# Second projections of a hybrid decoder trunk: all sums and low parts on VectorE, four of seven products' residuals on ScalarE and accumulating DMAs

## The chip, the core and the metric

The kernel runs on one core of one Trainium2 chip. The core has five engines that run their own instruction streams in order: TensorE (PE, with its weight loads shown apart as PEld), VectorE (DVE), ScalarE (ACT), GpSimd (POOL) and SyncE (SP, which here only issues DMAs). The metric is the device time of one execution in microseconds (us); lower is better. A profile is one execution of its own, with a span and times of single instructions.

## The reference

One sequence of 1024 tokens with 1024 features goes through two layers in float32. Each layer is a token mixer and a SwiGLU feed-forward network (FFN), each with an RMSNorm and a shift, scale and gate from the conditioning vector. The first mixer is a sparse attention with top-k keys, the second a gMLP.

```
for layer in range(2):
    h = modulate(rmsnorm(x, norm_mix_g[layer]), sh1, sc1)
    y = dsa_mixer(h, ...) if layer == 0 else gmlp_mixer(h, ...)      # both end in  "... @ w_o" / "y @ w_out"
    x = x + g1[:, None, :] * y
    h = modulate(rmsnorm(x, norm_ffn_g[layer]), sh2, sc2)
    x = x + g2[:, None, :] * ((silu(h @ w_gate) * (h @ w_up)) @ w_down)
return rmsnorm(x, final_g)
```

The change concerns the four *second projections* and the residual that follows each: `@ w_o` (1024 to 1024) of the attention, `@ w_down` (2816 to 1024) of the two FFNs, and `@ w_out` (2048 to 1024) of the gMLP, each with `x + gate * (...)`.

## The kernel before, in words

Activations are kept transposed: features on the 128 partitions, tokens along the row, in two chunks of 512 tokens. `x1` is eight tiles of 128x1024, one for each 128 output features.

**The second projections** all run through `out_win` (L1009). It computes a matrix product by Strassen's method in Winograd's form: the inner dimension, the output features and the tokens are each halved, and seven products take the place of eight. The inner dimension is cut into pieces: one piece of 4 for the attention (`[4]`), `[4, 4, 3]` for each FFN and `[4, 4]` for the gMLP; a piece of n covers 2n blocks of 128 inner features. For each piece, the seven products run in the order 1, 2, 6, 7, 4, 5, 3 (`ORD`, L1129). Each product has four output tiles (m = 0 to 3) of 128x512.

Precision is kept by splitting each operand in a high and a low part (`split`, L1056): ScalarE rounds to the high part, another engine subtracts it from the source to get the low part, and each block is three matmuls (`mm3`, L176: high by high, high by low, low by high). Product 2 of the first piece is an exception in the FFNs and the gMLP (`RAW_F`, L1106): it takes unsplit float32 operands. So a product of a piece of 4 is 4 x 4 x 3 = 48 matmuls of 128x512, and one of a piece of 3 is 36.

Ahead of the matmuls of a product come `mv_prep` (L1076, the moving side, from `graw` tiles) and `w_prep` (L1102, the weights, from `wraw` tiles). Between them they make, in a piece of 4: 28 low parts for the moving side and 28 for the weights (4 for each product), 16 sums for the moving side and 16 for the weights (all for products 6 and 7 and what follows from them). That is 88 subtractions or additions of 128x512 with both sources in SBUF, L1058 being all the low parts and L1084 to L1126 the sums. The tables at L88 to L91 say which of them go to GpSimd: `GS_P` and `WS_P` (indices whose sums do, moving side and weights), `GL_P` and `WL_P` (indices whose low parts do). With the values before, GpSimd takes 33 of the 88 and VectorE 55.

After the four output tiles of a product, the residual is added (`residual`, L950): VectorE reads the PSUM tile, multiplies by the gate and adds to the right eighth of `x1`. A product has four of these, a piece 28. Which part of `x1` a product goes to is told by `DST` (L1130): products 1 and 2 to features 0 to 511 of the first token chunk, 6 and 3 to the same features of the second chunk, 7 and 5 to features 512 to 1023 of the second chunk, 4 to those of the first. Products 1, 6, 7 and 4 share one group of four PSUM tiles (`X`), which goes on accumulating: TensorE may not write product 6 into a tile before the residual of product 1 has read it. Products 2 and 5, 3 use another group (`Z`).

Work is put on the engines in the order of the program text, rearranged by the framework's scheduler. Loads go on SP's DMA queue: the next piece's raw tiles are issued at products 4, 5 and 3 (`AHEAD`, L87). The weights' split tiles (`wst`) have eight buffers, so two products' worth: ScalarE can round the weights of a product only as TensorE ends the one two before. The pool `tmp` holds the short-lived 128x512 tiles named by `t2` (L132), four buffers.

The next stage's statistics and norm are interleaved with the last piece (L1170, L1334 and the like), and the first products of the next FFN or gMLP with that.

Of the kernel before, what the change touches and what calls it, by code (L numbers as in the profile page):

```python
# [14 lines left out]
AF = mybir.ActivationFunctionType  # L15
ALU = mybir.AluOpType
# [68 lines left out]
FIRST = ['13', '12', '11', '10', 'A0', 'A2', 'A3', 'A1', 'x0', 'x2', 'x3', 'x1', '21', '20', '23', 'p1', '22', 'B1', 'B0', 'B2', 'B3', 'x4', 'x6', 'x5', 'x7']  # L85
FIRST_O = ['13', '10', '11', 'A2', 'A3', 'x0', 'x3', 'A1', '12', 'x2', 'A0', 'x1', 'p1', '20', '23', 'B3', '21', 'B1', '22', 'B2', 'B0', 'x5', 'x4', 'x7', 'x6']
AHEAD = {4: [("A", i) for i in range(4)], 5: [("1", i) for i in range(4)], 3: [(w, i) for w in "2B" for i in range(4)]}  # L87
GS_P = (1,)  # L88
GL_P = (0, 2)
WS_P = (0, 2)  # L90
WL_P = (1,)  # L91
FM2 = (3,)
FORD = (6, 1, 7)
DGW = 1
# [19 lines left out]
def trunk(ctx, tc, xT, c, modT, vec, kgb, w_idx, w_q, w_a, wuk, wuv, wo, wg, wu, wd,  # L114
          bwu, bwv, bwo, bws, bbs, outT):
    nc = tc.nc
    PE, DVE, ACT, POOL, SP = nc.tensor, nc.vector, nc.scalar, nc.gpsimd, nc.sync
# [2 lines left out]
    pg = ctx.enter_context(tc.tile_pool(name="pg", bufs=37))  # L120
    wrp = ctx.enter_context(tc.tile_pool(name="wrp", bufs=2))
    wsp = ctx.enter_context(tc.tile_pool(name="wsp", bufs=8))
    tmp = ctx.enter_context(tc.tile_pool(name="tmp", bufs=4))
    sm = ctx.enter_context(tc.tile_pool(name="sm", bufs=4))
    psa = ctx.enter_context(tc.tile_pool(name="psa", bufs=4, space=PSUM))
    psb = ctx.enter_context(tc.tile_pool(name="psb", bufs=4, space=PSUM))
# [5 lines left out]
    def t2(name, dt=F32):  # L132
        return tmp.tile([P, CW], dt, name=name, tag="t2")
# [239 lines left out]
    for t in BEG:  # L373
# [8 lines left out]
        elif t[0] in "ab":  # L382
            k, ch = int(t[1]), int(t[0] == "b")
            cs = slice(ch * CW, ch * CW + CW)
# [77 lines left out]
    gate = [None]  # L462
# [90 lines left out]
    for ch in range(2):  # L553
        p = pa("kn_ps")
# [27 lines left out]
    for ch in range(2):  # L582
        p = pa("kT_ps")
# [363 lines left out]

    x1 = [None] * KT

    def residual(ps, xk, ch, gate, src=None):  # L950
        cs = slice(ch * CW, ch * CW + CW)
        DVE.scalar_tensor_tensor(xk[:, cs], ps, gate, (xk[:, cs] if src is None else src), op0=ALU.mult, op1=ALU.add)  # L952

    g_d = drm.tile([FT, P, T], F32, name="g_d")
# [54 lines left out]
    def out_win(src, wsrc, gate, x, pieces, xsrc=None, first=None, hook=None):  # L1009
# [66 lines left out]
        def mv_prep(pi, j):  # L1076
# [3 lines left out]
            for i in range(n):  # L1080
                (b11, b12), (b21, b22) = halves(pi, "1", i), halves(pi, "2", i)
                s = {1: b11, 2: b21, 7: b12, 4: b21, 5: b11, 3: b22}.get(j)
                if j == 6:
                    eng(GS_P, i).tensor_sub(b11, b12, b11)  # L1084
                    s = hold(("g", i)) if late else t2("gs")
                    eng(GS_P, i).tensor_sub(s, b22, b11)  # L1086
                if j == 7:
                    eng(GS_P, i).tensor_sub(b12, b22, b12)  # L1088
                if late and j == 4:
                    eng(GS_P, i).tensor_sub(b21, b21, keep.pop(("g", i)))  # L1090
                if j in whole(pi):
                    r.append(s)
                else:
                    t = pg.tile([P, 2, CW], F32R, name="gm", tag="pg")
                    r.append(split(t, s, CW, eng(GL_P, i)))
                if j == 6 and late:
                    keep["g", i] = s
                elif j == 6:
                    eng(GS_P, i).tensor_sub(b21, b21, s)
            return r  # L1100

        def w_prep(pi, j):  # L1102
# [3 lines left out]
            for m in range(4):  # L1106
                (a11, a22), (a12, a21) = halves(pi, "A", m, n), halves(pi, "B", m, n)
                s = {1: a11, 2: a12, 7: a11, 4: a22, 5: a21, 3: a12}.get(j)
                if j == 6:
                    eng(WS_P, m).tensor_sub(a11, a11, a21)  # L1110
                    s = (hold(("w", m)) if late else tmp.tile([P, CW], F32, name="wsum", tag="wt", bufs=2))[:, :n]
# [20 lines left out]
        def run():  # L1132
            fetch(len(todo))
            for pi, n in enumerate(pieces):
                last = pi == len(pieces) - 1
                if last:
                    for q in SQP:
                        sqpg[q] = page("sqp")
                        POOL.memset(sqpg[q][:, 0:1], 0.0)
                X = [pa("d_ps") for _ in range(4)]  # L1140
                Z = None
                for o, j in enumerate(ORD):
                    prep(pi, j)
                    if o < 6:
                        prep(pi, ORD[o + 1])
                    if last and o == 4:
                        prep(pi, 3)
                    if not last:
                        for what, i in AHEAD.get(j, ()):
                            if what in "AB" or i < pieces[pi + 1]:  # L1150
                                load(pi + 1, what, i)
                        if j == 3:
                            prep(pi + 1, 1)
                    if j in (2, 5):
                        Z = [pb("d_ps") for _ in range(4)]
                    mv, w = pre[pi, j]
                    mo, ch = DST[j]
                    for m in range(4):
                        p = (X if j in (1, 6, 7, 4) else Z)[m]
                        with (tc.issue_after(pe_chain[LOCK[n][j, m]].ins) if last and (j, m) in LOCK[n] else ExitStack()):  # L1160
                            for k in range(n):
                                first, end = k == 0 and j in (1, 2, 5), k == n - 1 and j in (2, 3, 4)
                                if j in whole(pi):
                                    PE.matmul(p, w[m][k], mv[k], start=first, stop=end, skip_group_check=j != 2)
                                else:
                                    mm3(p, w[m][k], mv[k], first, end, j != 2)
                        residual(p, x[m + mo], ch, gate[:, m + mo:m + mo + 1])
                    if hook is not None:
                        hook()
                    if last and j == 4:  # L1170
                        yield 0
            yield 1
# [428 lines left out]
    for ch in F1:  # L1601
        if ch is None:
            continue
        cs = slice(ch * CW, ch * CW + CW)
# [5 lines left out]
        for k in range(KT):  # L1610
            o = page("o")[:, :CW]
            x, fg = x1[k][:, cs], V[:, V_FIN + k:V_FIN + k + 1]
# [69 lines left out]
```

## Time and profile before

| | us |
|---|---|
| median of 3 runs (2596.45 to 2601.98) | 2601.79 |
| the profiled execution's own time | 2602.36 |
| its span | 2600.7 |

| second projection | stretch of the span, us | pieces |
|---|---|---|
| attention output | 525 to 645 | [4] |
| first FFN, down | 1084 to 1290 (its edges run from 1074 to 1317) | [4, 4, 3] |
| gMLP output | 1733 to 1890 (from 1721 to 1897) | [4, 4] |
| second FFN, down | 2344 to 2582 (from 2327 to 2584) | [4, 4, 3] |

In the tables of engines, "busy" is the time in which an engine had an instruction in execution, so an instruction that is held up while it executes counts as busy. PEclk is the share of its full clock that TensorE was granted. In the timelines, the first number is the start, the second the duration; instructions of one engine overlap by some 0.08 us, so that the pace of a row of them is the difference of their starts.

### The profile page before, as it was taken

How to read it: one execution, taken by the hardware profiler on the slowest of the kernel's cores; microseconds unless marked ns; L12 is line 12 of the kernel's file. 1: busy time of each engine (PE TensorE's matmuls, PEld its weight loads, DVE VectorE, ACT ScalarE, POOL GpSimd, SP SyncE). 2: the span in 40 equal slices, each digit the busy share in tenths (PEclk: the TensorE clock that was granted, in tenths of full speed). 3: DMA queues.
4: the chain of work that ended last, by engine and by line, in shares of the span. 5: the costliest groups of instructions: out<-in, count | busy, mean ns of one | idle time of the engine just before them, and what ended most of it. 6: DMA issues, size and time to landing. Idle time of an engine off the chain costs nothing. (4 is left out here: it accounts for less than half of the span.)

```text
span 2600.7 us, 31048 instructions
## 1 busy us (share of the span) xinstructions
PE 2397.1 (92%) x10254; PEld 1877.9 (72%) x10254; DVE 2133.6 (82%) x3433; ACT 1208.5 (46%) x2223; POOL 1344.0 (52%) x962
## 2 busy tenths in 40 slices
PE   6979889988899999989988999988999999999996
PEld 4544577876688888768766877767767888886785
DVE  6497988898988888799878688899889666568986
ACT  5377775655533333343464454424464333333334
POOL 2021143465755556665556455566467444455663
PEclk7999899999999999999998999999999999999998
DMA  6002265645135544632123244363132223254021
GB/s 255 33 9 74 107 212 177 231 134 163 60 133 186 193 164 154 251 130 97 37 78 122 81 142 131 108 259 130 50 113 98 105 98 111 76 213 162 14 98 65
DMA packets 133919, 328.58 MB, mean 126 GB/s; under 512 B 14080, under 2 KB 30720, under 8 KB 133760
## 3 DMA queue, kind: packets, MB, share of 16 engines
q1 hardware_dynamic: 130432, 318.22, 34.7%
q0 software_dynamic: 3328, 8.39, 1.1%
q8 instruction: 81, 1.33, 0.2%
q14 instruction: 78, 0.64, 0.1%
HBM read 253.16 MB, written 73.40 MB: 126 GB/s over the span
## 5 line engine op out<-in xcount | busy, mean ns | idle before, releaser
L1239 PE MATMUL p<-mv,wst 128*128 128x512 f32 x1232 | 484.8, 394 | 9.2 <-DVE mv L967 9.2
L1240 PE MATMUL p<-mv,wst 128*128 128x512 f32 x1232 | 484.3, 393 | 7.2 <-DVE wst L1218 7.2
L1238 PE MATMUL p<-mv,wst 128*128 128x512 f32 x1232 | 483.1, 394 | 2.4 <-ACT wst L1217 0.9
L1216 POOL TENSOR_TENSOR wsum<-wgu 128x512 f32<-128x512 f32 x208 | 300.4, 1447 | 303.2 <-DVE wst L1218 198.4
L179 PE MATMUL d_ps<-gm,wst 128*128 128x512 f32 x904 | 366.2, 406 | 50.5 <-DVE x L952 44.6
L181 PE MATMUL d_ps<-gm,wst 128*128 128x512 f32 x904 | 359.0, 397 | 2.0 <-DVE wst L1058 2.0
L180 PE MATMUL d_ps<-gm,wst 128*128 128x512 f32 x904 | 359.3, 397 | 0.2 <-DVE gm L1058 0.2
L1239 PEld LDWEIGHTS p<-mv,wst 128*128 128x128 f32 x1232 | 233.7, 190 | 63.1 <-DVE mv L967 13.8
L1240 PEld LDWEIGHTS p<-mv,wst 128*128 128x128 f32 x1232 | 234.0, 190 | 57.8 <-DVE wst L1218 9.4
L1238 PEld LDWEIGHTS p<-mv,wst 128*128 128x128 f32 x1232 | 233.9, 190 | 54.8 <-issue 2.5
L1217 ACT CAST wst<-wsum 128x512 fp32r<-128x512 f32 x260 | 161.3, 621 | 216.9 <-POOL wsum L1216 97.1
L179 PEld LDWEIGHTS d_ps<-gm,wst 128*128 128x128 f32 x904 | 174.1, 193 | 98.9 <-ACT wst L1057 32.6
L1218 DVE TENSOR_TENSOR wst<-wsum,wst 128x512 fp32r<-128x512 f32 x208 | 200.6, 966 | 44.4 <-ACT wst L1217 43.4
L952 DVE SCALAR_TENSOR_TENSOR x<-d_ps,modv,x 128x512 f32<-128x512 f32 x252 | 185.0, 740 | 30.7 <-PE d_ps L181 30.7
L181 PEld LDWEIGHTS d_ps<-gm,wst 128*128 128x128 f32 x904 | 174.1, 193 | 40.7 <-DVE wst L1058 3.2
L180 PEld LDWEIGHTS d_ps<-gm,wst 128*128 128x128 f32 x904 | 174.6, 193 | 38.9 <-issue 1.7
L1058 POOL TENSOR_TENSOR gm<-graw,gm 128x512 fp32r<-128x512 f32 x102 | 158.8, 1566 | 81.9 <-ACT gm L1057 67.4
L1057 ACT CAST wst<-wraw 128x512 fp32r<-128x512 f32 (+1 forms) x204 | 117.3, 593 | 160.1 <-PE d_ps L181 137.2
L1057 ACT CAST gm<-graw 128x512 fp32r<-128x512 f32 x192 | 113.1, 618 | 102.2 <-DVE wst L1058 34.2
L1058 DVE TENSOR_TENSOR wst<-wraw,wst 128x512 fp32r<-128x512 f32 (+1 forms) x153 | 133.8, 878 | 13.2 <-ACT wst L1057 13.2
L1058 POOL TENSOR_TENSOR wst<-wraw,wst 128x512 fp32r<-128x512 f32 (+1 forms) x51 | 72.9, 1430 | 126.7 <-ACT wst L1057 126.7
L1217 ACT CAST wst<-wgu 128x512 fp32r<-128x512 f32 x104 | 64.3, 619 | 144.0 <-PE p L1240 70.8
(380 smaller groups left out, 5576.9 us busy)
## 6 DMA issues: line engine op xcount, KB each, us to landing
md<-modT SPq DMA_DIRECT2D x96, 512.0 KB, 5.3
wgu<-wg SPq DMA_DIRECT2D x56, 512.0 KB, 3.5
wgu<-wu SPq DMA_DIRECT2D x56, 512.0 KB, 4.4
g_d<-uv SPq DMA_DIRECT2D x88, 256.0 KB, 2.0
graw<-g_d SPq DMA_DIRECT2D x44, 512.0 KB, 7.6
wraw<-wd SPq DMA_DIRECT2D x64, 256.0 KB, 6.4
x_d<-x SPq DMA_DIRECT2D x48, 256.0 KB, 2.1
x<-x_d SPq DMA_DIRECT2D x24, 512.0 KB, 7.1
```

What stands on the lines that cost most here:

```text
L179: PE.matmul(ps, sh, mh, start=first, stop=False, skip_group_check=run)
L180: PE.matmul(ps, sh, ml, start=False, stop=False, skip_group_check=run)
L181: PE.matmul(ps, sl, mh, start=False, stop=last, skip_group_check=run)
L952: DVE.scalar_tensor_tensor(xk[:, cs], ps, gate, (xk[:, cs] if src is None else src), op0=ALU.mult, op1=ALU.add)
L1057: ACT.copy(t[:, 0, :n], s)
L1058: e.tensor_sub(t[:, 1, :n], s, f(t[:, 0, :n]))
L1216: SUM_ENG[j].tensor_tensor(s, o[0], o[1], op=o[2])
L1217: ACT.copy(t[:, 0], s)
L1218: LO_ENG[j].tensor_sub(t[:, 1], s, f(t[:, 0]))
L1238: PE.matmul(ps, sh, mh, start=k == 0, stop=False)
L1239: PE.matmul(ps, sh, ml, start=False, stop=False)
L1240: PE.matmul(ps, sl, mh, start=False, stop=k == 3)
```

## The change

The four tables of GpSimd's part become empty, so that all 88 sums and low parts of a piece are VectorE's, in all four second projections. In the projections of more than one piece, the residuals of products 1, 2, 6 and 7 (in the last piece 1, 6 and 7) take another way: ScalarE reads the PSUM tile, multiplies by the gate and writes an SBUF tile `xadd`, and a DMA issued by GpSimd adds that tile to `x1` in place. The pool `tmp` goes from four buffers to ten, and the SBUF space for the descriptors of DMAs that GpSimd issues is set to 4096 bytes.

```diff
-GS_P = (1,)
-GL_P = (0, 2)
-WS_P = (0, 2)
-WL_P = (1,)
+GS_P = ()
+GL_P = ()
+WS_P = ()
+WL_P = ()
+FAR = (1, 2, 6, 7)
+FAR_L = (1, 6, 7)
...
-    tmp = ctx.enter_context(tc.tile_pool(name="tmp", bufs=4))
+    tmp = ctx.enter_context(tc.tile_pool(name="tmp", bufs=10))
...
-    def residual(ps, xk, ch, gate, src=None):
+    def residual(ps, xk, ch, gate, src=None, far=False):
         cs = slice(ch * CW, ch * CW + CW)
+        if far:
+            s = t2("xadd")
+            ACT.activation(s, ps, AF.Identity, scale=gate)
+            POOL.dma_start(xk[:, cs], s, accum_op=ALU.add)
+            return
         DVE.scalar_tensor_tensor(xk[:, cs], ps, gate, (xk[:, cs] if src is None else src), op0=ALU.mult, op1=ALU.add)
...
-                        residual(p, x[m + mo], ch, gate[:, m + mo:m + mo + 1])
+                        residual(p, x[m + mo], ch, gate[:, m + mo:m + mo + 1],
+                                 far=len(pieces) > 1 and j in (FAR_L if last else FAR))
...
-    nc = bacc.Bacc("TRN2", target_bir_lowering=False, num_devices=1)
+    nc = bacc.Bacc("TRN2", target_bir_lowering=False, num_devices=1, dynamic_dma_scratch_size=4096)
```

In numbers of instructions over the whole program: VectorE gets 288 two-source operations more and 116 residuals fewer, GpSimd 288 operations fewer and 116 DMA issues more, ScalarE 116 activations more. (Line numbers in the changed kernel are 2 to 8 higher: L952 becomes L959, L1058 becomes L1065.)

Three places in the middle piece of the first FFN's down projection show how the orders move. In the names, `x_8842`, `x_8848`, `x_8844`, `x_8846` are the tiles m = 0 to 3 of `x1`, and `x_8948`, `x_8952`, `x_8950`, `x_8954` the tiles 4 to 7; what stands in brackets is the engine or DMA queue whose semaphore the instruction waits for (DMAHW are SP's DMAs, DMASW GpSimd's).

First, VectorE at products 6 and 7. Before, low parts and residuals alternate:

```order
L952 SCALAR_TENSOR_TENSOR x_8842<-d_ps,modv_98,x_8842 128x512 [waits PE_49]
L1058 TENSOR_TENSOR wst<-wraw,wst 128x512 [waits Activation_49]
L952 SCALAR_TENSOR_TENSOR x_8848<-d_ps,modv_98,x_8848 128x512 [waits PE_49]
L1058 TENSOR_TENSOR gm<-graw,gm 128x512 [waits Activation_49]
L952 SCALAR_TENSOR_TENSOR x_8844<-d_ps,modv_98,x_8844 128x512 [waits PE_49]
L1058 TENSOR_TENSOR gm<-graw,gm 128x512 [waits Activation_49]
```

and with the change there are only sums and low parts at that place:

```order
L1119 TENSOR_TENSOR wsum<-wraw 128x512 [waits DVE_49] x2
L1132 TENSOR_TENSOR wraw<-wraw,wsum 128x512 [waits DVE_49] x2
L1065 TENSOR_TENSOR wst<-wsum,wst 128x512 [waits PE_49,Activation_49]
L1093 TENSOR_TENSOR gs<-graw 128x512 x4
L1065 TENSOR_TENSOR wst<-wsum,wst 128x512 [waits PE_49,Activation_49]
L1106 TENSOR_TENSOR graw<-graw,gs 128x512 [waits DVE_49] x2
L1065 TENSOR_TENSOR gm<-gs,gm 128x512 [waits Activation_49]
```

The residuals of products 1, 2, 6 and 7 are gone from VectorE's order, and the sums that GpSimd had made stand in it.

Second, GpSimd at the same place. Before:

```order
L1110 TENSOR_TENSOR wraw<-wraw 128x512 [waits DMAHW3_49,DVE_49]
L1112 TENSOR_TENSOR wsum<-wraw 128x512 [waits Pool_49]
L1126 TENSOR_TENSOR wraw<-wraw 128x512
L1058 TENSOR_TENSOR gm<-graw,gm 128x512 [waits DMAHW6_49,Activation_49]
L1058 TENSOR_TENSOR gm<-graw,gm 128x512 [waits DMAHW0_49,Activation_49]
```

and with the change, the issues of product 1, then those of product 2:

```order
L957 DMA x_8842<-xadd 128x512 [waits DMASW0_49,Activation_49]
L957 DMA x_8848<-xadd 128x512 [waits DMASW1_49,Activation_49]
L957 DMA x_8844<-xadd 128x512 [waits DMASW2_49,Activation_49]
L957 DMA x_8846<-xadd 128x512 [waits DMASW3_49,Activation_49]
L957 DMA x_8842<-xadd 128x512 [waits DMASW4_49,DMASW0_49,Activation_49]
L957 DMA x_8848<-xadd 128x512 [waits DMASW5_49,DMASW1_49,Activation_49]
```

GpSimd's whole order inside the projection is now such issues; the second DMA on a tile waits for the first.

Third, the changed kernel's VectorE at product 5, whose residual goes to the bytes that product 7's DMA adds to:

```order
L1091 TENSOR_TENSOR graw<-graw 128x512 [waits DVE_49]
L959 SCALAR_TENSOR_TENSOR x_8948<-d_ps,modv_98,x_8948 128x512 [waits DMASW4_49,PE_49]
L1095 TENSOR_TENSOR graw<-graw 128x512 [waits DMAHW6_49,DVE_49]
L1065 TENSOR_TENSOR wst<-wraw,wst 128x384 [waits Activation_49]
L1095 TENSOR_TENSOR graw<-graw 128x512 [waits DMAHW7_49,DVE_49]
L959 SCALAR_TENSOR_TENSOR x_8952<-d_ps,modv_98,x_8952 128x512 [waits DMASW5_49,PE_49]
```

The residual now waits for an accumulating DMA besides TensorE, and the sums and low parts of the next products stand behind it.

## The prediction

> **What bounds the kernel now.** I read the page's table of engines first, then the busy times by stretch, the waits of TensorE, and the timelines inside one projection. Over the whole span TensorE is nearly always busy, so any gain has to be sought where it is not:
>
> ```profile
> PE 2397.1 (92%) x10254; PEld 1877.9 (72%) x10254; DVE 2133.6 (82%) x3433; ACT 1208.5 (46%) x2223; POOL 1344.0 (52%) x962
> ...
> L179 PE MATMUL d_ps<-gm,wst 128*128 128x512 f32 x904 | 366.2, 406 | 50.5 <-DVE x L952 44.6
> ```
>
> The second row is the first matmul of each block of the second projections: 50.5 us of TensorE's idle time stand before it, 44.6 of them ended by a residual on VectorE. The busy times by stretch show the attention's projection, the three others, and 100 us inside the second FFN for comparison:
>
> ```profile
> core 0: us, PE busy (x) PEld busy (x) DVE busy (x) ACT busy (x) POOL busy (x), PEclk, DMA share, GB/s
> 525.00:645.00 120.00, 104.48 (x458) 82.05 (x456) 112.53 (x157) 61.81 (x113) 74.92 (x53) 0.96 0.44 146
> 1084.00:1290.00 206.00, 191.61 (x789) 150.65 (x788) 190.82 (x219) 81.01 (x145) 132.04 (x93) 0.98 0.26 92
> 1733.00:1890.00 157.00, 144.29 (x587) 111.17 (x586) 142.93 (x166) 66.06 (x115) 94.71 (x64) 0.98 0.27 98
> 2344.00:2582.00 238.00, 218.69 (x898) 171.80 (x896) 209.84 (x246) 93.99 (x167) 140.49 (x98) 0.96 0.20 73
> 2100.00:2200.00 100.00, 100.00 (x443) 82.82 (x442) 63.71 (x93) 38.70 (x66) 47.99 (x37) 1.00 0.29 100
> ```
>
> In the FFN TensorE runs without a gap at full clock, one matmul each 100/443 = 0.226 us; VectorE has 36% to spare. In the three long projections TensorE idles 14.4, 12.7 and 19.3 us, together 46.4, while VectorE is busy 88 to 93% of the time. The clock there is 0.98, 0.98 and 0.96, worth 0.02 x 206 + 0.02 x 157 + 0.04 x 238 = 16.8 us. The dips follow idle time, as three stretches of 20 us show:
>
> ```profile
> 2360.00:2380.00 20.00, 14.86 (x58) 10.46 (x56) 20.00 (x22) 7.37 (x14) 12.44 (x9) 0.93 0.01 2
> 2380.00:2400.00 20.00, 18.81 (x70) 15.29 (x71) 16.57 (x21) 8.86 (x16) 9.06 (x6) 0.82 0.74 265
> ...
> 2440.00:2460.00 20.00, 20.00 (x90) 16.57 (x89) 17.93 (x21) 8.12 (x15) 14.23 (x11) 1.00 0.00 1
> ```
>
> So **46.4 + 16.8 = 63 us** is the most that the three can give back. Why VectorE is late is seen in its timeline, 10 us of it, with GpSimd's row below:
>
> ```profile
> 1183.70 0.68 DVE L1058 TENSOR_TENSOR gm<-gs,gm 128x512 fp32r<-128x512 f32 x1
> 1184.31 0.74 DVE L952 SCALAR_TENSOR_TENSOR x<-d_ps,modv,x 128x512 f32<-128x512 f32 x1
> 1184.97 0.68 DVE L1058 TENSOR_TENSOR wst<-wsum,wst 128x512 fp32r<-128x512 f32 x1
> 1185.57 1.40 DVE L952 SCALAR_TENSOR_TENSOR x<-d_ps,modv,x 128x512 f32<-128x512 f32 x2
> ...
> 1190.06 1.78 DVE L1058 TENSOR_TENSOR wst<-wsum,wst 128x512 fp32r<-128x512 f32 x1
> 1191.76 1.78 DVE L1125 TENSOR_TENSOR wraw<-wraw,wsum 128x512 f32<-128x512 f32 x1
> 1193.47 1.78 DVE L1058 TENSOR_TENSOR gm<-graw,gm 128x512 fp32r<-128x512 f32 x1
> ...
> 1189.55 3.44 POOL L1058 TENSOR_TENSOR gm<-graw,gm 128x512 fp32r<-128x512 f32 x2
> ```
>
> Alone, a two-source operation takes 0.68 us and the next starts after 0.60 (1184.97 to 1185.57); a residual paces at 0.66 (1184.31 to 1184.97). While GpSimd works on tensors, the same operation takes 1.78 and paces at 1.70 (1190.06 to 1191.76), and GpSimd's own at 1.72: they go by turns. Each operation that GpSimd takes over from VectorE then costs VectorE 1.1 us of waiting, where doing it itself would cost 0.60. The residual, which reads PSUM, keeps its 0.74 beside GpSimd.
>
> **The change, part by part.** *Sums and low parts to VectorE.* In a middle piece of 4, VectorE will do 88 two-source operations at 0.60 and 12 residuals at 0.66: 52.8 + 7.9 = 60.7 us. TensorE needs 7 x 48 x 0.226 = 75.9 us for it. Before, the middle piece of the first FFN's projection had VectorE at
>
> ```profile
> 1140.00:1220.00 80.00, 76.25 (x327) 61.75 (x326) 73.70 (x81) 31.74 (x56) 50.92 (x33) 0.98 0.25 91
> ```
>
> 73.7 of 80 us for only 55 such operations and 28 residuals. The load falls from 92% to 80%; TensorE becomes the bound of first and middle pieces. Without the moved residuals it would be 52.8 + 28 x 0.66 = 71.3 of 75.9, nearly as tight as before; the two halves of the change need one another.
>
> What stays: the sums come in a burst. Products 6 and 7 need 32 sums and 16 low parts, 28.8 us of VectorE, to be spread over the 21.7 us of products 1 and 2 and what could be made ahead; and in a last piece statistics and norm join in on VectorE, where only 12 of 28 residuals are moved. I take **two thirds of 63, or 42 us**, as the gain, between 63 (no gap left) and 15 (bursts as bad as now in half of all places, the clock with them).
>
> *Residuals to ScalarE.* 116 activations from PSUM with a scale for each partition. The nearest rows are a PSUM copy and an activation with scale and bias:
>
> ```profile
> L1272 ACT COPY gu<-p 128x512 f32<-128x512 f32 x6 | 3.6, 592 | 0.0
> ...
> L973 ACT ACTIVATE hq<-xr,modv,asc 128x512 f32<-128x512 f32 x6 | 4.7, 808 | 0.0
> ```
>
> 0.59 to 0.81 us each; I take 0.6, the PSUM source being the nearer. The 44 in the first FFN's projection are 26 to 36 us of ScalarE, which has 206 - 81 = 125 us free there. What is queued behind: each stands ahead of the rounding of a weight tile that waits for the same matmul (two products' worth of `wst`), so it costs that rounding one 0.6 us in the 2.7 us between two output tiles. Nothing on the path, as that product is a whole one (10.8 us) ahead. TensorE's wait for the PSUM tile moves to ScalarE: product 7's first tile is due three output tiles, 8.1 us, after product 6's first is done. Zero; if VectorE's sums are late, though, ScalarE's roundings wait for them in order, and the 116 behind them.
>
> *Accumulating DMAs.* No such DMA is in the trace. GpSimd does issue ordinary ones in the attention:
>
> ```profile
> L817 POOL DMA_DIRECT2D rgk<-k_d x8: 706/746/936, 335.6 to 493.6; - x8
> ...
> L835 POOL DMA_DIRECT2D rgv<-v_d x8: 536/555/581, 336.5 to 450.0; - x8
> ...
> rgk<-k_d POOLq DMA_DIRECT2D x8, 512.0 KB, 4.2
> rgv<-v_d POOLq DMA_DIRECT2D x8, 512.0 KB, 5.8
> ...
> x_d<-x SPq DMA_DIRECT2D x48, 256.0 KB, 2.1
> ...
> DMA to landing us min/median/max: 2.0/4.1/8.5
> ```
>
> Issue: 0.54 to 0.94 us, taken as 0.75; four a product are 3.0 of 10.8 us on a GpSimd that has nothing else there. Landing: between 2.1 us (256 KB) and 8.5 (the last row: the slowest of the DMAs of `x`); I take 5, near the two GpSimd rows, whose 512 KB match a transfer of 256 KB that must read its target too. Who waits: the residual of product 5 on VectorE, for product 7's sum. It is due 1.25 products, 13.5 us, later (10.2 in a last piece); with 0.6 + 3.0 + 5 = 8.6 us it is in time. Product 3 has more room; in a last piece product 2's first residual comes 8.1 us after product 1's, whose own issue is first in its queue: 0.6 + 0.75 + 5 = 6.4. So zero, up to 8 us over all if landings are at 8.5. SP's loads are issued at products 4, 5 and 3, mostly away from these DMAs.
>
> The Trainium skill (DMA: Bandwidth & Descriptors, section "Anatomy of one DMA — SWDGE (gpsimd) path") gives 2.0 us plus bytes/436,000 for a DMA of GpSimd, an estimate of 2.6 us here; by it these waits are zero with more room, and no accumulating DMA is measured there.
>
> *The attention's projection* keeps its residuals on VectorE and takes 33 operations more: + 33 x 0.60 = 19.8 us. Its own get faster:
>
> ```profile
> L1058 DVE TENSOR_TENSOR wst<-wraw,wst 128x512 fp32r<-128x512 f32 x18 | 14.7, 814 | 0.0
> ...
> L1058 DVE TENSOR_TENSOR gm<-graw,gm 128x512 fp32r<-128x512 f32 x10 | 12.3, 1225 | 0.0
> ```
>
> from a mean of 0.96 to 0.68, or 55 x 0.28 = 15.4 us, and the statistics beside it somewhat. Zero, between 8 lost and 8 gained. More `tmp` buffers and less descriptor space: zero; the attention's and the FFNs' orders stay what they were.
>
> **Sum.** The profiled execution has 2602.4 us, 0.6 over the median of the runs; 2602.4 - 42 = 2560, which I give for the median as well.
>
> **Rivals.** *The bursts remain* (2582): VectorE's mean load falls, but TensorE stalls at products 6 and 7 as before, now behind a serial chain of sums on one engine; ScalarE, waiting for `wsum`, holds the roundings behind it. For it: 28.8 us of work for 21.7. Against: now it is (32 + 16) operations at a pace of up to 1.70. The gain is then a third of 63, some 20 us.
>
> *The issues and VectorE exclude each other, too* (2602): if a DMA issue took VectorE's turn as a tensor operation does, the middle piece would cost VectorE 60.7 + 16 x 0.75 = 72.7 us, against 73.7 before. Against it stands an issue inside a two-source operation, beside the median of that line:
>
> ```profile
> 474.76 1.22 DVE L246 SCALAR_TENSOR_TENSOR md<-md,cact 128x1024 f32<-128x1024 f32 x1
> ...
> 475.29 0.75 POOL L817 DMA_DIRECT2D rgk<-k_d  x1 [0.45 <-PE pt_ps L918]
> ...
> L246 DVE SCALAR_TENSOR_TENSOR md<-md,cact x89: 1191/1215/2303, 20.1 to 2183.4; 128x1024 f32<-128x1024 f32 x89
> ```
>
> 1.22 against 1.215, and 0.75 against 0.746: neither is stretched. The Trainium skill (SBUF — State Buffer, section "SBUF: two separate sides") warns that GpSimd cannot write a DMA's descriptors while VectorE runs an operation that takes both ports; by it the landings would be later. The row just shown speaks against it for two-source operations.
>
> *Late sums* (slower, 2610): accumulating may be far slower than copying. Place: product 5's residual on VectorE, with the next products' sums and low parts behind it. It decides from a landing of 13.5 - 3.6 = 9.9 us on; each microsecond over it is lost once in each of eight pieces, when VectorE has no slack left. To eat up the 42 us and 8 more takes 6.3 us a piece, a landing of 16 us, nearly twice the slowest row.
>
> **How the numbers follow.** The forecast, 2540 to 2578 around 2560: 0.53. More than that, toward 2602 - 63 - 8 = 2531: 0.10. Bursts remain: 0.20. Exclusion: 0.07. Late sums: 0.10. A measurement of this kernel can tell 0.2%, some 5 us. Faster: 0.53 + 0.10 + 0.20 and a little of the exclusion, 0.84. Same: 0.07. Slower: 0.09. The range runs from 2533 to 2604, leaving out the tail of late sums and the last of the best case.
>
> **What would show it.** Right: two-source operations in the projections at 0.68 us in mean, VectorE near 80% busy in the middle pieces, TensorE's idle time before L179 down from 50 to some 15 us, PEclk 1.00. Wrong: VectorE's residuals (L959) waiting for DMAs; operations of 1 us and more beside GpSimd's issues; issues well above 1 us; ScalarE's roundings waiting for `wsum` at products 6 and 7; the attention's projection longer than its 120 us.

## The result, and the profile after

The changed kernel takes 2534.55 us (median of four runs, 2528.32 to 2536.33), against 2601.89 of the kernel before beside it: a ratio of 0.9732, with a 95% interval of 0.9715 to 0.9749. It is **67 us faster, where 42 were forecast**. The median lies just inside the range of 2533 to 2604; measured by the ratio, 2601.79 x 0.9732 = 2532 us, it is a microsecond below it. Either way it is the "more than that" case, to which the prediction had given 0.10.

The page's table of engines and the first matmul of each block of the second projections, after:

```profile
PE 2375.1 (94%) x10254; PEld 1868.0 (74%) x10254; DVE 2035.7 (80%) x3605; ACT 1271.9 (50%) x2339; POOL 1011.5 (40%) x790
...
L181 PE MATMUL d_ps<-gm,wst 128*128 128x512 f32 x904 | 355.0, 397 | 5.9 <-DVE x L959 5.2
```

TensorE's idle time before these matmuls fell from 50.5 to 5.9 us. VectorE has 172 instructions more and is busy 98 us less.

Where the time came from is read by stretches that go exactly from the first to the last matmul of a projection: first FFN, gMLP, second FFN, attention. Before:

```profile
1074.20:1315.60 241.40, 226.07 (x942) 178.61 (x941) 221.07 (x258) 99.13 (x175) 150.93 (x106) 0.98 0.31 110
1720.20:1899.70 179.50, 166.79 (x683) 129.72 (x683) 165.43 (x196) 76.90 (x133) 110.56 (x74) 0.98 0.34 125
2334.20:2581.00 246.80, 228.49 (x941) 179.92 (x939) 218.75 (x254) 95.58 (x170) 149.28 (x103) 0.96 0.23 86
532.70:637.50 104.80, 92.79 (x398) 73.26 (x397) 97.57 (x138) 53.26 (x96) 63.42 (x46) 0.97 0.37 121
```

After (the columns are the stretch, its length, busy time and instructions of PE, PEld, DVE, ACT and POOL, the granted clock, the DMA share and GB/s):

```profile
1071.30:1291.90 220.60, 219.66 (x942) 175.96 (x941) 186.59 (x308) 123.29 (x219) 48.48 (x54) 1.00 0.64 173
1697.80:1856.60 158.80, 158.66 (x674) 125.48 (x673) 138.57 (x223) 93.34 (x161) 41.56 (x43) 1.00 0.63 180
2292.00:2512.60 220.60, 219.66 (x941) 175.62 (x939) 182.13 (x302) 120.12 (x214) 47.99 (x53) 1.00 0.57 148
533.40:633.50 100.10, 93.21 (x403) 75.26 (x402) 94.66 (x164) 51.09 (x92) 21.34 (x17) 0.95 0.38 122
```

The three long projections are shorter by 20.8, 20.7 and 26.2 us, 67.7 together; the attention's by 4.7. What lies outside them is 4.2 us longer over all, and the profiled execution is 68.2 us shorter (2602.4 to 2534.2). About 2 us of the gMLP's part only moved: nine matmuls of neighbouring work stood inside its stretch before (x683) and stand outside it now (x674). In the three long ones TensorE is now busy almost without a gap (2.0 us of idle time in 600) at the full clock: what is left in them is the matmuls' own time.

The same projection of the first FFN by its pieces, before and then after:

```profile
1074.20:1166.90 92.70, 84.38 (x327) 63.16 (x326) 87.70 (x94) 33.02 (x57) 66.20 (x42) 0.96 0.45 167
1166.90:1245.30 78.40, 76.95 (x337) 62.84 (x336) 72.56 (x83) 31.19 (x55) 48.32 (x37) 1.00 0.23 81
1245.30:1315.60 70.30, 64.74 (x280) 52.62 (x280) 60.82 (x83) 34.92 (x63) 36.41 (x29) 0.98 0.19 68
```

```profile
1071.30:1151.70 80.40, 80.40 (x327) 61.22 (x326) 71.17 (x116) 41.72 (x73) 15.80 (x17) 1.00 0.82 243
1151.70:1227.90 76.20, 76.20 (x338) 63.07 (x337) 62.95 (x105) 39.92 (x70) 14.25 (x19) 1.00 0.55 138
1227.90:1291.90 64.00, 63.06 (x280) 51.68 (x279) 52.47 (x89) 41.66 (x76) 18.43 (x18) 1.00 0.51 124
```

The first piece gave 12.3 us, the last 6.3, the middle one 2.2. VectorE's load in the middle piece, from which the prediction argued, was 72.56 of 78.40 us, and yet hardly anything was lost there. In the first piece VectorE's 87.70 us were more than the 80.40 that TensorE needs when nothing holds it up (the length after).

VectorE's low parts of the moving side, before, and after:

```profile
L1058 DVE TENSOR_TENSOR gm<-graw,gm 128x512 fp32r<-128x512 f32 x90 | 102.2, 1141 | 9.2 <-ACT gm L1057 9.0
```

```profile
L1065 DVE TENSOR_TENSOR gm<-graw,gm 128x512 fp32r<-128x512 f32 x192 | 126.1, 687 | 5.6 <-ACT gm L1064 5.5
```

VectorE makes 192 instead of 90 for 23.9 us more. Over the three long projections it executes 833 instructions in 507 us (308 + 223 + 302; 186.59 + 138.57 + 182.13), before 708 in 605. Last, the moved residuals, by line: ScalarE's part, GpSimd's issue with its landing, and what VectorE's own residuals waited for:

```profile
L956 ACT ACTIVATE xadd<-d_ps,modv x116: 669/690/695, 1080.3 to 2485.1; 128x512 f32<-128x512 f32 x116
...
L957 POOL DMA_DIRECT2D x<-xadd x116: 869/869/1232, 1081.3 to 2486.1; - x116
...
DMA to landing us min/median/max: 3.2/3.8/10.8
...
L959 DVE SCALAR_TENSOR_TENSOR x<-d_ps,modv,x x136: 729/744/752, 538.4 to 2514.9; 128x512 f32<-128x512 f32 x136
...
  PE d_ps L183: 31.7, 30
```

No residual of VectorE waited for a landing.

### The profile page after: what moved, and what is told of

The parts are those of the page before. It is cut to its first block, busy times and chain, and to the rows that moved or that the text cites. A ratio compares the mean times of both kernels' runs of the same rounds, so it can differ in the third digit from the quotient of the medians.

```text
span 2532.4 us, 31279 instructions
## 1 busy us (share of the span) xinstructions
PE 2375.1 (94%) x10254; PEld 1868.0 (74%) x10254; DVE 2035.7 (80%) x3605; ACT 1271.9 (50%) x2339; POOL 1011.5 (40%) x790
## 4 chain that ended last, share of the span: by engine, by line
PE 65%; DVE 20%; issue 5%; DMA 5%; POOL 3%; ACT 3%; SPq 0%; DVEq 0%; POOLq 0%; ACTq 0%
PE p L1246 9%; PE p L1247 9%; PE p L1248 9%; PE d_ps L181 7%; PE d_ps L183 7%; PE d_ps L182 7%; DVE sc L702 2%; PE q_ps L468 2%; PE d_ps L1171 2%; DVE wst L1226 2%; DMA md<-modT 1%; DVE mv L974 1%; PE qi_ps L408 1%; PE z_ps L181 1%; PE z_ps L182 1%
## 5 line engine op out<-in xcount | busy, mean ns | idle before, releaser
L1247 PE MATMUL p<-mv,wst 128*128 128x512 f32 x1232 | 484.6, 394 | 13.4 <-DVE mv L974 13.4
L181 PE MATMUL d_ps<-gm,wst 128*128 128x512 f32 x904 | 355.0, 397 | 5.9 <-DVE x L959 5.2
L182 PE MATMUL d_ps<-gm,wst 128*128 128x512 f32 x904 | 352.4, 391 | 0.0
L183 PE MATMUL d_ps<-gm,wst 128*128 128x512 f32 x904 | 351.5, 391 | 0.0
L957 POOL DMA_DIRECT2D x<-xadd x116 | 101.4, 889 | 372.2 <-ACT xadd L956 299.2
L1226 DVE TENSOR_TENSOR wst<-wsum,wst 128x512 fp32r<-128x512 f32 x208 | 208.2, 1003 | 49.9 <-ACT wst L1225 49.4
L181 PEld LDWEIGHTS d_ps<-gm,wst 128*128 128x128 f32 x904 | 170.6, 189 | 45.5 <-issue 7.9
L182 PEld LDWEIGHTS d_ps<-gm,wst 128*128 128x128 f32 x904 | 170.7, 189 | 37.4 <-issue 2.2
L183 PEld LDWEIGHTS d_ps<-gm,wst 128*128 128x128 f32 x904 | 170.5, 189 | 36.0
L1065 DVE TENSOR_TENSOR wst<-wraw,wst 128x512 fp32r<-128x512 f32 (+1 forms) x204 | 132.2, 655 | 57.5 <-ACT wst L1064 57.0
L1226 POOL TENSOR_TENSOR wst<-wgu,wst 128x512 fp32r<-128x512 f32 x52 | 75.5, 1453 | 138.5 <-ACT wst L1225 80.1
L1065 DVE TENSOR_TENSOR gm<-graw,gm 128x512 fp32r<-128x512 f32 x192 | 126.1, 687 | 5.6 <-ACT gm L1064 5.5
L959 DVE SCALAR_TENSOR_TENSOR x<-d_ps,modv,x 128x512 f32<-128x512 f32 x136 | 101.0, 744 | 31.8 <-PE d_ps L183 31.7
```

Source lines behind the costliest of these rows:

```text
L181: PE.matmul(ps, sh, mh, start=first, stop=False, skip_group_check=run)
L182: PE.matmul(ps, sh, ml, start=False, stop=False, skip_group_check=run)
L183: PE.matmul(ps, sl, mh, start=False, stop=last, skip_group_check=run)
L957: POOL.dma_start(xk[:, cs], s, accum_op=ALU.add)
L1065: e.tensor_sub(t[:, 1, :n], s, f(t[:, 0, :n]))
L1226: LO_ENG[j].tensor_sub(t[:, 1], s, f(t[:, 0]))
```

## The experiments

Ratios are to the kernel before, run beside each on the same chip. The theories are named as in the expectations: A, VectorE's mean load decides; B, TensorE waits for a residual that stands behind sums and low parts in VectorE's order; C, the turns with GpSimd cost the time. Four more arose on the way: D, GpSimd's DMA issues take VectorE's turns; E, ScalarE's added work makes the loss; F, GpSimd's work in other stages is beside the path; G, accumulating and its landings make the loss.

### Each half of the change alone

Only the tables emptied:

```diff
-FAR = (1, 2, 6, 7)
-FAR_L = (1, 6, 7)
+FAR = ()
+FAR_L = ()
```

> The sums and low parts go to VectorE, all residuals stay there too. Theory A (VectorE's load decides, the two halves need one another): in a middle piece VectorE has 71.3 of 75.9 us, nearly as tight as before; the gain is a third of the changed kernel's 68 us, some 20 us: 2582 us. Theory B (TensorE waits for a residual that stands behind sums and low parts in VectorE's order; moving the residual cures it): the residuals still stand there, TensorE's idle time before the first matmul of the blocks stays above 30 us, gain 0 to 25 us: 2577 to 2602. Theory C (the turns with GpSimd alone cost the time): without them most comes back, 45 us and more: under 2557.

Measured: 2544.69 us, ratio 0.9781 (0.9759 to 0.9804), some 57 us faster. Only the residuals moved, the tables as before:

```diff
-GS_P = ()
-GL_P = ()
-WS_P = ()
-WL_P = ()
+GS_P = (1,)
+GL_P = (0, 2)
+WS_P = (0, 2)
+WL_P = (1,)
```

> GpSimd keeps its share of the sums and low parts, and the residuals go by ScalarE and accumulating DMAs. Theory A: VectorE's load falls from 221 of 241 us in the first FFN's projection by 44 x 0.66 = 29 us, as much as the other half takes away, but GpSimd now has tensor work and 44 issues of 0.9 us; a third of the gain, some 20 to 30 us: 2572 to 2582. Theory B: the wait for the residual goes, TensorE's idle time before the blocks falls from 50 to under 20 us, and 40 to 60 us come back: 2542 to 2562. Theory C: the turns remain, gain under 15 us: above 2587.

Measured: 2636.65 us, ratio 1.0130 (1.0111 to 1.0149), **34 us slower than before**, which no theory had. The three projections in the tables-only kernel:

```profile
1063.60:1290.00 226.40, 222.11 (x942) 177.08 (x941) 212.78 (x352) 99.93 (x175) 10.14 (x11) 0.99 0.33 118
1697.90:1861.50 163.60, 158.89 (x672) 125.23 (x671) 156.77 (x254) 75.91 (x131) 17.65 (x14) 1.00 0.38 133
2294.00:2518.00 224.00, 219.90 (x941) 175.50 (x939) 208.77 (x346) 95.83 (x170) 9.08 (x9) 1.00 0.27 95
```

VectorE executes 952 instructions in 578 us, 244 more than before in 27 us less. Of GpSimd's 283 instructions in these stretches before (106 + 74 + 103), 34 are left; the other 249 had not relieved VectorE at all. The 244 are 146 us of work at 0.60 each, so 173 us of waiting went with GpSimd's 249: 0.7 us for each, a little more than doing it. VectorE is 93 to 96% busy, more than the 89 to 92% of before, but now nearly all of it is work, and TensorE loses 14 us (614.0 against 600.0) where it had lost 67.7. Set against the 600 us that TensorE needs, VectorE's time was 605 us before and is 578 here. Theory C stands, and the figures of A and B fail for the main effect.

Two things stay beside it. GpSimd's own sums and low parts may also have come late. In the kernel before no wait of TensorE's matmuls in these stages was ended by GpSimd, but ScalarE waited 42 us for its sums (`wsum`) and VectorE 12 for its low parts; the run below in which GpSimd makes neither sums nor low parts and still costs time speaks for the turns. And what B describes is left as a small part: 7.7 us of TensorE's idle time over the whole span still end with such a residual, against 5.2 in the changed kernel:

```profile
PE d_ps L181 <- DVE x L959: 7.7, 5, 2.6
```

### Why the residuals alone made it slower

In the timeline of the residuals-only kernel, VectorE and then GpSimd, inside the first piece of the gMLP's projection:

```profile
1757.11 1.58 DVE L1119 TENSOR_TENSOR hs<-wraw 128x512 f32<-128x512 f32 x1
1758.61 15.40 DVE L1133 TENSOR_TENSOR wraw<-wraw 128x512 f32<-128x512 f32 x1
1773.93 5.48 DVE L1065 TENSOR_TENSOR gm<-graw,gm 128x512 fp32r<-128x512 f32 x1
...
1758.09 0.87 POOL L957 DMA_DIRECT2D x<-xadd  x1
1758.70 1.56 POOL L1065 TENSOR_TENSOR gm<-hs,gm 128x512 fp32r<-128x512 f32 x1
1759.93 1.55 POOL L1117 TENSOR_TENSOR wraw<-wraw 128x512 f32<-128x512 f32 x1
1761.14 1.18 POOL L957 DMA_DIRECT2D x<-xadd  x1
...
1771.54 1.83 POOL L1065 TENSOR_TENSOR wst<-wraw,wst 128x512 fp32r<-128x512 f32 x1
```

A VectorE operation that needs 0.68 us lasts 15.40, while GpSimd does eleven tensor operations, mostly at a pace of 1.22 us, without a turn for VectorE. In the kernel before, no two-source operation of VectorE in the three projections lasted over 1.81 us. Here 31 do, and every one of them overlaps an issue of GpSimd; the one shown begins during an issue and ends during another. Two variants of the residuals-only kernel tell the issue from the rest. First, no issue (the residuals of the moved products are then not added at all):

```diff
             ACT.activation(s, ps, AF.Identity, scale=gate)
-            POOL.dma_start(xk[:, cs], s, accum_op=ALU.add)
             return
```

> The residuals-only kernel (2636.7 us), whose 116 accumulating DMAs are left out: ScalarE still makes the scaled tile, but the residuals of the moved products are not added anywhere. Theory D (the issues between GpSimd's tensor operations take VectorE's turns away; there VectorE's two-source operations took 543 us in the three projections, against 486 before): without the issues they fall back to 490 us or less, and the time to that of before or below, 2570 to 2600 us. Theory E (the loss comes from ScalarE's added work and from the order of the roundings behind it): the loss stays, 2625 to 2640.

Measured: 2591.11 us, ratio 0.9947 (0.9928 to 0.9965). The loss is gone while ScalarE's added work is still there, so theory E falls. Taking 116 residuals from VectorE is worth only 14 us while the turns remain. This run also shows that VectorE's load alone does not set the time: it is busy for 542 us here, less than in the tables-only kernel, and yet the three projections take 649.5 us, 49.5 more than in the changed kernel. TensorE's longest waits there are for ScalarE's part of the moved residuals (14.3 us), VectorE's low parts (10.2) and VectorE's residuals (9.3). Beside GpSimd's tensor work, results come late even from a VectorE with time to spare; by which chain is not separated.

Second, a plain copy to HBM in place of the accumulation (`spare` holds 116 tiles in HBM that nobody reads):

```diff
-            POOL.dma_start(xk[:, cs], s, accum_op=ALU.add)
+            POOL.dma_start(spare.pop(), s)
```

> The residuals-only kernel (2636.7 us), whose accumulating DMAs are replaced by plain ones: GpSimd copies the scaled tile to a spare place in HBM, one for each, which nobody reads; the moved residuals are not added anywhere. Theory D (an issue of GpSimd between its tensor operations takes VectorE's turns): as slow as with accumulating, 2620 to 2645 us, against 2591 without any issue. Theory G (accumulating into x, its landing or its waits make the loss): as without issues, 2582 to 2600.

Measured: 2604.77 us, ratio 0.9994 (0.9978 to 1.0009): between the two. By the ratios, the issues cost 48 us (1.0130 against 0.9947): 12 what plain ones cost, and 35 more for accumulating. With plain issues the longest of VectorE's two-source operations in the projections lasts 6.75 us. The low parts of VectorE (the group shown of before, x90, 1141 ns) follow in the same order: none, plain, accumulating:

```profile
L1064 DVE TENSOR_TENSOR gm<-graw,gm 128x512 fp32r<-128x512 f32 x90 | 104.3, 1169 | 20.7 <-ACT gm L1063 20.7
```

```profile
L1066 DVE TENSOR_TENSOR gm<-graw,gm 128x512 fp32r<-128x512 f32 x90 | 109.2, 1227 | 10.0 <-ACT gm L1065 9.8
...
L958 POOL DMA_DIRECT2D spare<-xadd x116: 540/557/592, 1096.4 to 2560.6; - x116
```

```profile
L1065 DVE TENSOR_TENSOR gm<-graw,gm 128x512 fp32r<-128x512 f32 x90 | 135.0, 1513 | 12.7 <-ACT gm L1064 12.5
...
L957 POOL DMA_DIRECT2D x<-xadd x116: 867/1000/3087, 1081.5 to 2589.6; - x116
```

So an issue among GpSimd's tensor operations takes turns away from VectorE, and the longer accumulating one takes more (theory D); no wait of VectorE's residuals for a landing appears in that kernel either, which speaks against G. Theory D had expected the plain issue to be as bad as the accumulating one, and it is not; why the accumulating issue weighs more than its length (0.87 us against 0.56 undisturbed) stays open.

### The same residuals by a tensor operation of GpSimd

```diff
-            POOL.dma_start(xk[:, cs], s, accum_op=ALU.add)
+            POOL.tensor_add(xk[:, cs], xk[:, cs], s)
```

> The changed kernel (2534.6 us), but the tile that ScalarE has scaled is added to x by a tensor operation of GpSimd, not by an accumulating DMA. Theory C (each operation that GpSimd does costs VectorE 1.1 us of turns): 116 x 1.1 = 128 us more for VectorE in 600 us of projections in which it is 85% busy; it runs over by 6% and more, 36 us or more lost: 2570 to 2600 us, slower than with all residuals on VectorE (2544.7), where they cost 116 x 0.66 = 77 us. Theory B (the place of the residual in VectorE's order decides): as good as the changed kernel, 2530 to 2542.

Measured: 2568.54 us, ratio 0.9857 (0.9831 to 0.9882), 34 us slower than with the DMAs, a little under theory C's figure and far from B's. It is slower than leaving these residuals on VectorE (0.9781): 116 operations put back on GpSimd cost more than they save. VectorE is busy for 598 us in the three projections instead of 507, with the same work: 0.8 us for each of the 116. Not all of the loss need be turns: ScalarE also waits 18.6 us there for GpSimd's additions to free the `xadd` tiles. VectorE's moving low parts, 687 ns in the changed kernel, are back at

```profile
L1065 DVE TENSOR_TENSOR gm<-graw,gm 128x512 fp32r<-128x512 f32 x192 | 164.8, 888 | 5.1 <-ACT gm L1064 5.1
```

### Is it VectorE's load? 106 operations more

```diff
+                        if len(pieces) > 1 and m % 2 == 0 and j not in whole(pi):
+                            z = t2("xadd")
+                            DVE.tensor_sub(z, f(mv[0][0]), f(mv[0][1]))
                         residual(p, x[m + mo], ch, gate[:, m + mo:m + mo + 1],
```

> The changed kernel (2534.6 us) with 106 more two-source operations on VectorE in the three long projections, two for each product that isn't made whole, whose results nobody reads: 106 x 0.60 = 64 us of 600, so that VectorE is some 95% busy instead of 85%. Leaving the moved residuals on VectorE adds 116 x 0.66 = 77 us and cost 10 us (2544.7). Theory A (VectorE's load makes those 10 us): 64/77 of it, 6 to 10 us lost: 2541 to 2545. Theory B (the place of the residuals in VectorE's order makes them): extra work that nobody waits for costs less, 2533 to 2539.

Measured: 2538.67 us, ratio 0.9754 (0.9736 to 0.9771), which against the changed kernel's interval is no clear difference. The three projections:

```profile
1071.50:1292.20 220.70, 219.62 (x942) 176.03 (x942) 206.45 (x344) 122.56 (x219) 48.68 (x55) 1.00 0.63 173
1700.10:1860.70 160.60, 158.62 (x673) 125.49 (x672) 152.00 (x248) 93.02 (x161) 41.55 (x43) 1.00 0.64 181
2300.50:2521.50 221.00, 219.65 (x941) 175.59 (x939) 204.32 (x342) 120.00 (x214) 48.10 (x53) 1.00 0.56 148
```

VectorE is busy 563 of 602 us, 93%, and the projections are only 2.3 us longer than in the changed kernel. With the residuals on VectorE (the tables-only kernel) it is 94% busy, and they are 14 us longer. In the traces that leans towards B, but it does not settle the smaller effect. By the runs this kernel and the tables-only one are not clearly apart (0.9736 to 0.9771 and 0.9759 to 0.9804 overlap), VectorE has 15 us less to do here (563 against 578), and of the 13 us that TensorE idles in the tables-only projections only 4.4 end with a residual. What makes the smaller effect stays open.

### How far are the landings from the path? Two of each

Each of the two adds half of the residual (`half` is half the gate):

```diff
-            POOL.dma_start(xk[:, cs], s, accum_op=ALU.add)
+            for _ in range(2):
+                POOL.dma_start(xk[:, cs], s, accum_op=ALU.add)
...
+                        far = len(pieces) > 1 and j in (FAR_L if last else FAR)
-                        residual(p, x[m + mo], ch, gate[:, m + mo:m + mo + 1],
-                                 far=len(pieces) > 1 and j in (FAR_L if last else FAR))
+                        residual(p, x[m + mo], ch, (half if far else gate)[:, m + mo:m + mo + 1], far=far)
```

> The changed kernel, each moved residual added in two halves by two accumulating DMAs of the same tile, the second after the first. Issue and landing of one had a median of 0.87 and 3.8 us, the slowest landing 10.0; VectorE's own residual is due 13.5 us after the product. Two take about 9.3 us: if the landings were as far off the path as the trace says, nothing changes, 2530 to 2540 us. If the slowest ones (20 us in two) are waited for, once in each of the eight pieces up to 6 us: 2540 to 2580.

Measured: 2561.88 us, ratio 0.9834 (0.9814 to 0.9855), 27 us slower. GpSimd waits for the first of two to land before it issues the second, and so the queue falls behind: from the end of ScalarE's part to the last landing, the median over the 116 rises from 4.2 to 11.5 us and the slowest from 11.1 to 37.4. Now VectorE's residuals wait; in the first FFN's projection:

```profile
DVE x L960 <- DMA x<-xadd: 12.2, 3, 7.0
```

The rival "late sums" had the right place: VectorE's residual of product 5 is due after 13.5 us, and all six waits of VectorE for these landings in this kernel stand before the first residual of a product 5. In the changed kernel none of the 116 takes that long, here 49 do. The median's margin is large, that of the slowest is not.

### The attention's projection

Its tables as before, or its residuals of products 1, 6 and 7 moved as well:

```diff
-            return POOL if i in tab else DVE
+            return POOL if i in tab and len(pieces) == 1 else DVE
```

> The changed kernel, but the attention's projection keeps GpSimd's share of sums and low parts. The prediction had put that part of the change at zero, between 8 lost and 8 gained; the traces show its projection 4.7 us shorter (104.8 to 100.1). If that comes from the change: 2534.5 + 4.7 = 2539 us. If it is the variation of one execution: 2534.5, within 2 us.

```diff
-                                 far=len(pieces) > 1 and j in (FAR_L if last else FAR))
+                                 far=j in (FAR_L if last else FAR))
```

> The changed kernel, and the attention's projection sends its residuals of products 1, 6 and 7 by ScalarE and accumulating DMAs, too. In the changed kernel TensorE idles 6.9 us there, 3.3 of them before a block, ended by a residual, and its clock is 0.95 over 100 us. Theory A and B alike: at most 3.3 us plus a part of the 5 us of the clock come back: 2527 to 2533 us. If the accumulating DMAs queue behind the loads of the attention's stretch: no gain, 2534 to 2540.

Measured: 2545.44 us, ratio 0.9778 (0.9756 to 0.9800), and 2530.25, ratio 0.9719 (0.9698 to 0.9740). The first is slower than the changed kernel by some 11 us, more than either expectation: its projection takes 106.3 us instead of 100.1, the rest is not located, and the two intervals (0.9756 to 0.9800 and 0.9715 to 0.9749) only just stay apart. The second is no clear difference in all, though its projection is shorter in the trace (94.0 us instead of 100.1).

### The rule carried on: GpSimd's work of the other stages

The kernel just shown, with the attention's residuals moved as well (2530.25 us), and in the first projections of the FFNs and the gMLP all sums, low parts and norm parts on VectorE too:

```diff
-    SUM_ENG = {1: POOL, 2: POOL, 5: DVE, 6: POOL, 7: POOL}
-    LO_ENG = {1: DVE, 2: DVE, 3: DVE, 4: POOL, 5: DVE, 6: DVE, 7: POOL}
-    UA_ENG = POOL
-    VL_ENG = POOL
+    SUM_ENG = {j: DVE for j in range(1, 8)}
+    LO_ENG = {j: DVE for j in range(1, 8)}
+    UA_ENG = DVE
+    VL_ENG = DVE
...
-                B[2].append(part(a_, None, None, None, POOL if k % 2 else DVE))
-                B[4].append(part(c_, ALU.subtract, a_, POOL, POOL if k % 2 else DVE))
+                B[2].append(part(a_, None, None, None, DVE))
+                B[4].append(part(c_, ALU.subtract, a_, DVE, DVE))
...
```

> The kernel with the attention's projection changed too (2530.3 us), and GpSimd's sums and low parts of the first projections and of the gMLP go to VectorE as well. Theory C (turns cost VectorE 1.1 us for each operation of GpSimd, doing it itself 0.6): VectorE's load falls there too, and a part of the some 50 us in which TensorE idles at the starts of these stages comes back: 2500 to 2525 us. Theory F (there TensorE is bound already, and GpSimd's work was beside the path): 2526 to 2535. If the sums now stand in VectorE's order behind others and come late: above 2540.

Measured: 2501.32 us, ratio **0.9603 (0.9580 to 0.9627)**, faster than the changed kernel and the one it varies, and inside theory C's range; F falls. From its page:

```profile
PE 2370.0 (95%) x10254; PEld 1868.7 (75%) x10254; DVE 2115.6 (84%) x4092; ACT 1286.9 (51%) x2351; POOL 283.7 (11%) x303
...
L1247 PE MATMUL p<-mv,wst 128*128 128x512 f32 x1232 | 484.4, 393 | 3.3 <-DVE mv L974 3.3
```

VectorE executes 659 instructions more than the kernel before and is busy 18 us less. In the changed kernel the second row had been

```profile
L1247 PE MATMUL p<-mv,wst 128*128 128x512 f32 x1232 | 484.6, 394 | 13.4 <-DVE mv L974 13.4
```

so that TensorE's wait for VectorE's low part there fell from 13.4 to 3.3 us. That is 10 of the 29 us gained; the rest is not located. Two variants of it: the attention's low parts to VectorE as well (four lines of the attention with `DVE` in place of `POOL`), and without the moved residuals (`FAR = ()`, `FAR_L = ()`).

> The kernel with VectorE everywhere (2501.3 us), and the low parts of the attention's queries, weights, keys and probabilities, some 65 operations of GpSimd, go to VectorE, too. Theory C: they cost VectorE 1.1 us of turns each at most, and 0.6 done by itself; VectorE's load from 300 to 525 us (87%) falls or stays, a few us gained: 2490 to 2501. If VectorE is seldom in turns there and its order is the bound: 2501 to 2515.

> The kernel with VectorE everywhere (2501.3 us), with all residuals back on VectorE and no accumulating DMA. With GpSimd's tensor work gone from the projections, the moved residuals were worth 10 us (2544.7 against 2534.6); the same here: 2508 to 2516 us. If VectorE's load is what they relieve, and it is higher now at the stages' ends: more than 2516.

Measured: 2494.01 us, ratio 0.9563 (0.9533 to 0.9592), and 2517.34, ratio 0.9652 (0.9627 to 0.9678). The first is inside theory C's range, but its interval still touches that of the kernel that it varies, and it has no usable profile (the profiled execution took 6058.64 us, the five others 2487 to 2502; the cause isn't known). The second shows the accumulating DMAs still worth some 13 us by the ratios, 16 by the medians, at the edge of its two expectations.

## Why the prediction was right and wrong

- **The mechanism was right, its price too high.** Forecast: an operation of GpSimd costs VectorE 1.1 us of waiting, doing it oneself 0.60. The 1.1 holds where two operations meet; over the projections it was 0.7 us (tables only) and 0.8 us (GpSimd adds). Forecast were two-source operations at 0.68 us in mean; measured 0.687 in the moving low parts, and 0.655 in those of the weights, some of which are only 128x384. The middle piece's 60.7 of 75.9 us on VectorE became 62.95 of 76.20.
- **The step that failed is "two thirds of 63, or 42 us".** The whole bound came back: the three projections gave 67.7 us. The third was withheld for the burst of sums at products 6 and 7, 28.8 us of work in 21.7 "and what could be made ahead". The part made ahead was never sized. In the trace after, with low parts and blocks paired in order, the FFNs' middle pieces have the low parts for products 1 and 2 ready 12 us or more before their use, more than the 28.8 - 21.7 = 7.1 us by which the burst overruns; at product 6 the lead is down to 5 us (3 in their last pieces), and TensorE waits for none of them. The burst was also counted too large: 12 of the 32 sums (L1106, L1132 and L1133 of the changed kernel) feed products 4, 5 and 3, so products 6 and 7 need 20 sums and 16 low parts, 36 x 0.60 = 21.6 us. And the work was counted against the wrong place: the middle piece, where VectorE had 72.6 us to do in the 76.2 that TensorE needs, gave 2.2 of the 20.8 us; the first piece, with 87.7 in 80.4, gave 12.3.
- **The bound of 63 was itself a little low.** The stretches cut off the edges of the projections, so that the clock's part was 16.8 us; over the full stretches above it is 0.02 x 241.4 + 0.02 x 179.5 + 0.04 x 246.8 = 18.3, with 46.3 idle 64.6 in all. Of the last 3 us, 2 are the nine matmuls that moved out of the gMLP's stretch (9 x 0.226), and the rest is within the rounding of the clock to two digits.
- **"The two halves need one another" was wrong.** One half alone brings 57 us, the other alone costs 34. VectorE's 71.3 of 75.9 us (94%) without the moved residuals were read as nearly as tight as before. Measured, the tables-only projections lose 14 us at 94% and the kernel with the added operations 2 at 93%, where the kernel before lost 67.7 at 91%: much of that share was time held up beside GpSimd, which counts as busy.
- **ScalarE and the issues:** 0.69 us instead of 0.6, and 0.87 instead of 0.75; both were hidden, as forecast.
- **Landings:** 3.8 us in the median against 5 taken, the slowest 10.8 against 8.5; no wait, as forecast. Doubling them shows that the place of "late sums" was right too.
- **The exclusion rival** was answered from one row, an issue on a GpSimd without tensor work. For the changed kernel that holds (moving low parts at 687 ns with 116 issues beside them). For the residuals-only kernel it does not.
- **The attention's projection**, put at zero, gave 4.7 us in the trace and some 11 by the runs, beyond the bound of 8 gained, though the runs' intervals do not exclude it.

## What to carry to other kernels

A busy share does not tell work from waiting for a turn: compare the duration of an operation with its duration alone, and multiply the difference by the count, before an engine is called full. Set its time against the time that TensorE needs in that piece, not against the length that the waits have already stretched. Two-source work given from VectorE to GpSimd can cost VectorE more than it saves, so test the opposite of sharing; here it paid in the second projections and again in the first ones. When work is gathered on one engine, size the lead that the queue already has against the burst, by stage, and hold no discount back without it.

## What the runs showed of the hardware

- An operation of GpSimd's own tensor work stretched VectorE's two-source operation (128x512) from 0.68 to at most 1.81 us in the kernel before, by turns. With DMA issues among GpSimd's tensor operations the turns failed: 31 of VectorE's two-source operations took longer, one of them 15.40 us. DMA issues alone, without tensor work beside them, stretched nothing: 208 of VectorE's operations in the changed kernel overlap an issue and no tensor operation of GpSimd, and none of them took over 0.70 us.
- The Trainium skill (SBUF — State Buffer, section "SBUF: two separate sides") says that the pair of ports shared by the two engines is locked for a whole instruction, the first to come getting it. The turns of 1.70 us agree with that. Eleven operations of GpSimd in a row past a waiting VectorE do not follow from it.
- The issue of an accumulating DMA of 256 KB from SBUF to SBUF took 0.87 us and landed in 3.8 us (median), a plain one from SBUF to HBM 0.56 and 2.4.
- The three long projections run with 2.0 us of gaps at a granted clock of 1.00; before, with gaps of up to 6.3 us and 46.3 in all, it was 0.96 to 0.98, and some 18 of the 67.7 us were the clock.
